# Where the sample groups of a hybrid decoder step keep their states: four buffers, two of them in the GDN chains' scratch memory

## The chip, the cores and the metric

The kernel runs on one core of a Trainium2 chip. The metric is the time of one execution on the device, in microseconds (us): the median over runs. The core has five engines with a queue of instructions each, worked off in order: PE (TensorE, matrix products; the load of a product's stationary side is listed apart as PEld), DVE (VectorE), ACT (ScalarE), POOL (GpSimd), and SP (SyncE), which here issues nearly all DMAs.

## The reference

One layer of a decoder serves two groups of sequences with the same weights: a prompt of 1024 tokens behind 16 learned meta tokens, and 8 samples of one new token each, which carry cached states.

```python
u = rms_norm(x) @ w_in                     # 1024 -> 8216 columns
q_m, k_m, v_m, o_m, z_m, i_m, f_m, q_g, k_g, v_g, z_g, b_g, a_g = split(u)
(C, n, m), hm = chunked(mlstm_chunk, ...)  # 4 heads, state 128 x 256 each
ym = head_rms(hm) * w_mnorm * sigmoid(o_m) * silu(z_m)
qkv = silu(causal_conv(q_g | k_g | v_g))   # width 4
S, og = chunked(gdn_chunk, ...)            # 8 heads, state 128 x 128 each
yg = head_rms(og) * w_gnorm * silu(z_g)
x = x + concat(ym, yg) @ w_out             # 2048 -> 1024
y = rms_norm(x)
```

Both mixers keep a state per head that is handed from chunk to chunk. mLSTM: `C` is scaled by a decay and gets `k` times `v`; the output is `q @ C` and a normaliser. GDN (gated DeltaNet): `S` is scaled by a decay and gets a correction, `k` times (`v` less what `S` holds for `k`), which needs a triangular solve in each chunk. For a sample the chunk is one token: every sample's state (`state_gdn_S`: 8 samples x 8 heads x 128 x 128, `state_mlstm_C`: 8 x 4 x 128 x 256) is read, multiplied with the new `k` and `q`, decayed, changed by one outer product and written back. The outputs are the two groups' rows and all the new states.

## The kernel before

**Work on PE.** The main stream are the projections `u`: tiles of 128 columns of `w_in`, each over three blocks of about 350 tokens, each 24 matmuls of 128 x 350 (weights and input are split into a high and a low part in a fast format, so three products for one). They carry the names `pjg` (GDN), `pjm` (mLSTM), `pjz`, `pjo`, `pjzm` (gates); the generator that emits them is called the filler. At the end comes the output product `op`: seven products of half the size in each direction with 96 matmuls each (a fast matrix scheme, `PRODUCTS`), whose right sides are sums of blocks of `w_out` (`right_sums`: on POOL for the first four, on DVE for the others), split into two parts (`owh` by ACT, `owl` by DVE) and whose results are added into the rows `xr` or `regionxl` on DVE (`drain`). A product's bank is used again two products later, once its additions are done.

**Chains.** Between the projections stand the chains, one head after the other: GDN heads 0 to 7 (`gdn_chain`, products `tp`, `sk`, `up`), then mLSTM heads 0 to 3 (`mlstm_chain`: `mtp`, `mup`, `mnm`), each nine chunks. A step of a GDN chain makes small 128 x 128 tiles in turn: `vt`, `R`, `qs`, `wv`, the state `S`, the output `oo`. Each kind has its own small ring of tiles (`w(tag, ...)`). While a GDN chain runs, `query_squares` squares the head's queries in four pieces on ACT, into the first half of `srow`; DVE transposes each into the second half and sums it.

**Samples.** One generator, `samples`, does the GDN samples and then the mLSTM samples. `gdn_sample` takes the heads in pairs. A state of one head for all 8 samples is a tile of 128 x 1024 (512 KB), and two such tiles are in use, `db` and `ebuf[0]`, which the GDN chains used until then. For a pair: products `sA` of both states with `k` and `q` (16 matmuls, 8 for each state), POOL decays the states, ACT copies the result to `srow`, PE turns it (`sT`), DVE works out the correction, PE turns that (`svt`), it goes to memory and comes back broadcast to all partitions (`vb`), and DVE adds the outer products, 8 instructions for each state. Then `exchange` stores a state and loads the next one into the same tile. `mlstm_sample` does the same in a simpler form with `mqc`, `mqT` and the last sum `mms`, for four heads of two tiles each.

**Weights of the output.** `places` names the memory for the 16 blocks of `w_out` as it comes free: two tiles of the weights' ring, two of the ring `r_gm`, the two `ebuf` once the samples are done, then the region of the input, which is free when the last projection is done.

**What sets the order.** The program is written out by a planner (`Plan`) when it is built. Every generator yields a tile that it waits for, a condition, or an engine, and the planner, with a cost for each instruction and DMA, keeps a clock for each engine and always goes on with the first generator in its list whose wait is over by PE's clock. What comes out is a fixed order for each engine. The waits between engines are semaphores, so at run time an engine stands still where another is later than the planner thought.

Of the kernel before, what the change touches and what calls it, by code (L numbers as in the profile page):

```python
# [286 lines left out]
ORDERS = ((2, 3, 0, 1), (0, 1, 2, 3), (2, 3, 0, 1), (2, 3, 0, 1))  # L287
# [20 lines left out]
def hymba_kernel(ctx: ExitStack, tc: tile.TileContext, a: dict, o: dict):  # L308
# [17 lines left out]
    def room(tag):  # L326
        return plan.room(tag, BANKS[tag])
# [149 lines left out]
    wnames = {}  # L477

# [579 lines left out]
    def gdn_chain(h):  # L1058
# [8 lines left out]
        def prepare(c):  # L1067
# [9 lines left out]
            vt = w("vt", [P], f"vt{h}_{c}")  # L1077
# [11 lines left out]
        for c in range(NCH):  # L1089
# [5 lines left out]
            if c > 0:  # L1095
                pe.matmul(sk[:, P : 2 * P], kc, S, start=True, stop=True)
                pe.matmul(tp[:, 3 * P : 4 * P], qc, S, start=True, stop=True)
                R = w("R", [P], f"R{h}_{c}")
                dve.scalar_tensor_tensor(
                    out=R, in0=sk[:, P : 2 * P], scalar=negc[:, c, h : h + 1], in1=vt, op0=ALU.mult, op1=ALU.add)  # L1100
                qs = w("qs", [P], f"qs{h}_{c}")
# [5 lines left out]
            wv = w("wv", [P], f"wv{h}_{c}")  # L1107
# [7 lines left out]
            Sn = w("S", [P], f"S{h}_{c}", bufs=3)  # L1115
            if c == 0:
                dve.tensor_copy(Sn, up[:, 0:P])
            else:
                dve.scalar_tensor_tensor(
                    out=Sn, in0=S, scalar=egend[:, c, h : h + 1], in1=up[:, 0:P], op0=ALU.mult, op1=ALU.add)  # L1120
                oo = w("oo", [P], f"oo{h}_{c}", 3)
# [32 lines left out]

    def query_norms():

        yield squares
        yield room("k")
        pt = pst2("qsum")
        pe.matmul(pt[:, 0 : 32 * GH], fold, squares.rearrange("p h b -> p (h b)"), start=True, stop=True)  # L1160
        yield pt
        for r in range(4):
            rows = slice(32 * r, 32 * r + 32)
            part = pt[rows, 0 : 32 * GH].rearrange("p (h c r) -> p h c r", h=GH, r=4)[:, :, :, r]
            dve.scalar_tensor_tensor(out=hst[rows, MH : MH + GH, :], in0=part, scalar=EPS * MDK, in1=hst[rows, MH : MH + GH, :], op0=ALU.mult, op1=ALU.add)

    def store(place, o_):

        yield r_gm.can
        turns[0] += 1  # L1170
        ti, turn = r_gm.get([D], f"turn{turns[0]}")
# [9 lines left out]

    turns = [0]
# [31 lines left out]

    def exchange(t, to, source, key):
# [3 lines left out]
        if source is not None:  # L1219
            yield plan.read[t.tensor.name]  # L1220
# [4 lines left out]
    def gdn_sample():  # L1225
# [57 lines left out]
        vbs = ebuf[1], vb  # L1283
        for h in range(0, GH, 2):
            yield lambda: h == 0 or ("sS", h) in done and ("sS", h + 1) in done
            for x in (*sb, kn):
                yield x
            yield room("k")
            at = pst2(f"sA{h}")
            for i in range(2):  # L1290
                for b in range(NS):
                    g, j = divmod(b, 4)
                    g = P * (g + 2 * i)
                    pe.matmul(at[32 * j : 32 * j + 32, g : g + P], knf[:, 16 * h : 16 * h + 32], sb[i][:, b, :], start=True, stop=True)
            for i in range(2):
                pool.tensor_tensor(out=sb[i], in0=sb[i], in1=eg[:, h + i].unsqueeze(2).to_broadcast([P, NS, P]), op=ALU.mult)
            yield at
            for i in range(2):
                act.copy(srow[:, 256 * i : 256 * i + 256], at[:, 256 * i : 256 * i + 256])
            yield srow  # L1300
            yield room("k")
            turned = pst2(f"sT{h}")
            for g in range(4):
                pe.transpose(turned[:, P * g : P * g + P], srow[:, P * g : P * g + P], ident)
            yield turned
            for i in range(2):
                hi = h + i

                def of(k):
                    c = 272 * i + 8 * k  # L1310
                    return turned[:, c : c + 33 * NS - 32 : 33]

                dve.tensor_tensor(out=sn[:, 3, hi], in0=of(0), in1=eg[:, hi], op=ALU.mult)
                dve.scalar_tensor_tensor(out=sn[:, 3, hi], in0=vv[:, hi], scalar=0.5, in1=sn[:, 3, hi], op0=ALU.mult, op1=ALU.subtract)
                dve.tensor_tensor(out=sn[:, 3, hi], in0=sn[:, 3, hi], in1=bet[:, hi], op=ALU.mult)
                dve.tensor_tensor(out=sn[:, 4, hi], in0=of(1), in1=eg[:, hi], op=ALU.mult)
                dve.tensor_tensor(out=sn[:, 5, hi], in0=sn[:, 3, hi], in1=r[:, 5, hi], op=ALU.mult)
                dve.tensor_tensor(out=sn[:, 4, hi], in0=sn[:, 4, hi], in1=sn[:, 5, hi], op=ALU.add)
            yield sn
            yield room("k")  # L1320
            vp = pst2(f"svt{h}")
            pe.transpose(vp[0 : 2 * NS, 0:P], sn[:, 3, h : h + 2].rearrange("p h b -> p (h b)"), ident)
            vsb = wk.tile([2 * NS, P], F32, tag="vsb", name=f"vsb{h}")
            act.copy(vsb, vp[0 : 2 * NS, 0:P])
            sp.dma_start(vb_d[8 * h : 8 * h + 16], vsb)
            for i in range(2):
                sp.dma_start(vbs[i], vb_d[8 * (h + i) : 8 * (h + i) + 8].partition_broadcast(P))
            for i in range(2):
                hi, s_, vb = h + i, sb[i], vbs[i]
                yield s_  # L1330
                yield vb
                for b in range(NS):
                    if b % 2 == 0:
                        yield "dve"
# [914 lines left out]
```

## Time and profile before

| | |
|---|---|
| median of three runs | 1180.1 us (1176.85 to 1181.13) |
| profiled execution | 1178.63 us |
| its span, first to last instruction | 1176.8 us |
| PE busy | 1154.7 us (98%) |
| DVE, ACT, POOL busy | 893.3, 589.0, 466.3 us |
| mean granted clock of PE | 0.997 |
| DMA | 171.63 MB, 146 GB/s in the mean |

An engine's busy time is the time in which an instruction of it ran. PE's matmuls overlap each other and the weight loads, so that busy PE is not PE at its peak. A row of the timeline gives the start from the span's beginning, the duration, the engine, and what was written and read, and in brackets how long the engine had been idle just before and what it waited for. Names are those of the program without numbers. Every instruction carries line 56, that of the recording wrapper, so tiles and not lines tell them apart.

### The profile page before, as it was taken

The numbers are of one execution on the slowest core, as the hardware profiler recorded it, in microseconds if no ns is written. First come the engines' busy times: TensorE is split into PE (matmuls) and PEld (weight loads), VectorE is DVE, ScalarE is ACT, GpSimd is POOL, SyncE is SP. The second block draws the span as 40 slices with busy tenths as digits, with TensorE's granted clock in tenths as the row PEclk, the third lists the DMA queues.
The fourth block names the chain that finished last, engine by engine and source line by source line (L and its number), as shares of the span: only waits on it lengthen the run. The fifth ranks groups of instructions, "written<-read, shape, count | busy, mean of one in ns | idle before, by whom it ended". The sixth has DMA issues, their size and how long they took to land.

```text
span 1176.8 us, 22725 instructions
## 1 busy us (share of the span) xinstructions
PE 1154.7 (98%) x8049; PEld 1080.7 (92%) x8049; DVE 893.3 (76%) x2324; ACT 589.0 (50%) x1814; POOL 466.3 (40%) x644
## 2 busy tenths in 40 slices
PE   8999999999999999999999999999999999989997
PEld 7999999999999999999999989899999999866885
DVE  6789878598887879887664856457868776897886
ACT  6544445566565555655454655456432222433443
POOL 3104877855748295958311341320011111530012
PEclk9999999999999999999999999999999999999999
DMA  6032311313122223022412557667798988873342
GB/s 247 16 101 71 95 51 50 105 55 90 44 81 62 80 66 85 26 69 80 130 69 69 170 179 220 195 208 263 242 342 282 354 303 322 285 257 119 111 157 85
DMA packets 94460, 171.63 MB, mean 146 GB/s; under 512 B 28025, under 2 KB 53841, under 8 KB 94346
## 3 DMA queue, kind: packets, MB, share of 16 engines
q1 hardware_dynamic: 94152, 170.01, 44.0%
q8 instruction: 63, 1.03, 0.4%
q14 instruction: 51, 0.42, 0.1%
q10 hardware_dynamic: 194, 0.17, 0.1%
HBM read 116.04 MB, written 54.10 MB: 145 GB/s over the span
## 4 chain that ended last, share of the span: by engine, by line
PE 82%; DVE 8%; DMA 5%; issue 2%; ACT 1%; SPq 1%; POOL 1%; DVEq 0%; POOLq 0%; ACTq 0%
PE pjg L56 22%; PE pjm L56 10%; PE op L56 9%; PE pjz L56 8%; PE pjo L56 7%; PE pjzm L56 7%; PE up L56 4%; PE tp L56 3%; PE sk L56 2%; PE mnm L56 2%; PE mup L56 2%; PE kk L56 1%; SPq L56 1%; DVE owl L56 1%; PE xtp L56 1%
## 5 line engine op out<-in xcount | busy, mean ns | idle before, releaser
L56 PE MATMUL pjg<-xht,whg 128*128 128x350 f32 (+6 forms) x624 | 197.3, 323 | 1.0 <-ACT xht L56 1.0
L56 PE MATMUL pjg<-xlt,whg 128*128 128x350 f32 (+6 forms) x624 | 196.7, 322 | 0.0
L56 PE MATMUL pjg<-xht,wlg 128*128 128x350 f32 (+6 forms) x592 | 190.3, 325 | 0.0
L56 POOL TENSOR_TENSOR tmp<-B,E 33x31 f32<-33x31 f32 (+15 forms) x248 | 146.8, 592 | 73.8 <-DMA B<-nd 55.0
L56 POOL TENSOR_TENSOR E<-E,tmp 33x31 f32<-33x31 f32 (+15 forms) x248 | 155.7, 628 | 19.4
L56 PE MATMUL op<-owh,left 128*128 128x512 f32 x448 | 141.7, 395 | 4.0 <-DVE xr L56 4.0
L56 PE MATMUL pjm<-xht,whm 128*128 128x350 f32 (+2 forms) x384 | 127.5, 332 | 0.0
L56 PE MATMUL pjm<-xht,wlm 128*128 128x350 f32 (+2 forms) x384 | 126.7, 330 | 0.0
L56 PE MATMUL pjm<-xlt,whm 128*128 128x350 f32 (+2 forms) x384 | 126.1, 328 | 0.0
L56 PEld LDWEIGHTS pjg<-xht,whg 128*128 128x128 f32 x624 | 116.4, 189 | 1.6 <-issue 1.2
L56 PEld LDWEIGHTS pjg<-xlt,whg 128*128 128x128 f32 x624 | 116.4, 189 | 0.4
L56 PEld LDWEIGHTS pjg<-xht,wlg 128*128 128x128 f32 x592 | 110.9, 189 | 0.5
L56 PEld LDWEIGHTS op<-owh,left 128*128 128x128 f32 x448 | 84.1, 188 | 26.7 <-DVE xr L56 5.3
L56 DVE SCALAR_TENSOR_TENSOR kq<-cr,prm,kq 128x346 f32<-128x346 f32 (+7 forms) x147 | 96.2, 660 | 10.8 <-ACT cr L56 5.2
L56 PE MATMUL op<-owl,left 128*128 128x512 f32 x224 | 88.5, 395 | 0.0
L56 POOL TENSOR_TENSOR db<-db,sgb 128x1024 f32<-128x1024 f32 x8 | 15.4, 1922 | 167.2 <-PE mqc L56 90.6
L56 PEld LDWEIGHTS pjm<-xht,whm 128*128 128x128 f32 x384 | 72.8, 190 | 0.6 <-ACT who L56 0.2
L56 PEld LDWEIGHTS pjm<-xht,wlm 128*128 128x128 f32 x384 | 72.7, 189 | 0.5 <-issue 0.2
L56 PEld LDWEIGHTS pjm<-xlt,whm 128*128 128x128 f32 x384 | 72.8, 190 | 0.4 <-issue 0.2
L56 ACT COPY cr<-pjg 128x3 f32<-128x3 f32 (+8 forms) x124 | 40.5, 326 | 51.5 <-PE pjg L56 51.3
L56 PE MATMUL pjz<-xht,wlz 128*128 128x344 f32 x192 | 62.8, 327 | 0.0
L56 PE MATMUL pjz<-xht,whz 128*128 128x344 f32 x192 | 62.8, 327 | 0.0
(367 smaller groups left out, 3126.6 us busy)
## 6 DMA issues: line engine op xcount, KB each, us to landing
wrg<-in_wt SPq DMA_DIRECT2D x23, 512.0 KB, 3.9
left<-c_d SPq DMA_DIRECT2D x40, 256.0 KB, 2.7
wrm<-in_wt SPq DMA_DIRECT2D x16, 512.0 KB, 6.5
h_d<-turn SPq DMA_DIRECT2D x64, 128.0 KB, 3.7
ht<-h_d SPq DMA_DIRECT2D x16, 512.0 KB, 6.4
gm<-rows_d SPq DMA_DIRECT2D x8, 576.0 KB, 5.6
xt<-in_x_p SPq DMA_DIRECT2D x8, 512.0 KB, 5.4
wrz<-in_wt SPq DMA_DIRECT2D x8, 512.0 KB, 3.4
```

Source lines behind the costliest of these rows:

```text
L56: r = f(*args, **kw)
```

## The change

1. One tile `small` of sixteen pieces of 128 x 128 takes the place of the chains' six small rings; `piece(tag)` hands the pieces out in turn, in the same numbers as the rings had. The last two pieces are the second buffer for `query_squares`: its pieces 1 and 3 are written there, 0 and 2 to `srow` as before.
2. When the last GDN chain is done, the first sixteen pieces become two state tiles of 128 x 1024 (`pairs_of_pieces`). `gdn_sample` then runs two lanes: one takes heads 0, 1, 4, 5 through `db` and `ebuf[0]`, the other heads 2, 3, 6, 7 through the two halves of `small`. Each lane has one buffer for the broadcast corrections instead of two for all. `sample_banks` keeps the lanes from holding both PSUM banks of their kind, and `rows_held` gives `srow` to one lane at a time.
3. `mlstm_sample` loads the states of two heads at its start, into the four tiles, and a freed tile gets the state two heads on.
4. `places` names `ebuf[0]`, the two halves of `small` and `ebuf[1]` first, each as soon as the mLSTM samples have left it. Eight blocks instead of ten then go to the input's region.
5. `ORDERS[2]`: mLSTM head 2 projects queries and keys ahead of its values.

```diff
-ORDERS = ((2, 3, 0, 1), (0, 1, 2, 3), (2, 3, 0, 1), (2, 3, 0, 1))
+ORDERS = ((2, 3, 0, 1), (0, 1, 2, 3), (0, 1, 2, 3), (2, 3, 0, 1))
...
+    small = gp.tile([P, 16, P], F32, name="small")
+    plan.split(small, P)
+    plan.war.add(small.tensor.name)
+    PIECES, turns = dict(vt=(0, 2), wv=(2, 2), S=(4, 3), R=(7, 2), qs=(9, 2), oo=(11, 3)), {}
+
+    def piece(tag):
+        first, n = PIECES[tag]
+        turns[tag] = k = turns.get(tag, -1) + 1
+        return small[:, first + k % n, :]
...
-            vt = w("vt", [P], f"vt{h}_{c}")
+            vt = piece("vt")
...
-            sq, turned = srow[:, 0 : 2 * P], srow[:, 2 * P : 4 * P]
+            sq = small[:, 14:16, :].rearrange("p a b -> p (a b)") if i % 2 else srow[:, 0 : 2 * P]
+            turned = srow[:, 2 * P : 4 * P]
...
+    held, rows_held = [0], set()
+    pairs_of_pieces = [small[:, 8 * i : 8 * i + 8, :] for i in range(2)]
+
+    def sample_banks():
+        return held[0] < 2
...
-        sb = (db, ebuf[0])
-        for i in range(2):
-            yield plan.read[sb[i].tensor.name]
-            sp.dma_start(sb[i], a["s_S"][i])
+        def lane(first, sb, vb):
+            for i in range(2):
+                yield plan.read.get(plan.key(sb[i]), 0.0)
+                sp.dma_start(sb[i], a["s_S"][first + i])
+                done.add(("sS", first + i))
+            for h in range(first, GH, 4):
+                yield lambda: ("sS", h) in done and ("sS", h + 1) in done and ("C", GH - 1) in done
...
+                for i in range(2):
+                    hi, s_ = h + i, sb[i]
+                    yield plan.read.get(plan.key(vb), 0.0)
+                    sp.dma_start(vb, vb_d[8 * hi : 8 * hi + 8].partition_broadcast(P))
...
+                    plan.add(exchange(s_, o["s_S"][hi], a["s_S"][hi + 4] if hi + 4 < GH else None, ("sS", hi + 4)))
+            done.add(("lane", first))
+
+        plan.add(lane(0, (db, ebuf[0]), ebuf[1]), SAMPLE)
         yield lambda: ("C", GH - 1) in done and r_gm.can()
         gi, vb = r_gm.get([NS, P], "svb")
         yield plan.read[vb.tensor.name]
...
+        plan.join(small)
+        plan.split(small, D)
+        plan.add(lane(2, pairs_of_pieces, vb), SAMPLE)
+        yield lambda: ("lane", 0) in done and ("lane", 2) in done
...
+        states = db, ebuf[0], *pairs_of_pieces
+        for n in range(4):
+            yield plan.read.get(plan.key(states[n]), 0.0)
+            sp.dma_start(states[n], a["s_C"][n // 2, n % 2])
+            done.add(("sC", n))
...
+            sb = [states[(2 * h + i) % 4] for i in range(2)]
...
-                plan.add(exchange(s_, o["s_C"][h, i], a["s_C"][h + 1, i] if h + 1 < MH else None, ("sC", h + 1, i)))
+                plan.add(exchange(s_, o["s_C"][h, i], a["s_C"][h + 2, i] if h + 2 < MH else None, ("sC", n + 4)))
...
+        for n, t in enumerate((ebuf[0], *pairs_of_pieces, ebuf[1])):
+            yield has("sC", min(9 + n, 11))
+            yield plan.read[plan.key(t)]
+            yield t.rearrange("p a b -> p (a b)")
...
-        yield has("samples")
-        for e in ebuf:
-            yield e.rearrange("p a b -> p (a b)")
```

What moves on the engines, at three places of the written order. First ScalarE, at the start of GDN head 6's chain: the third and fourth square of head 5, the evacuation of a projection, and the first `vt`. Before:

```order
L56 ACTIVATE cr_358_7132<-kq_6598 128x346
L56 ACTIVATE srow<-kq_4976 128x256 x2
L56 ACTIVATE mv_2_7280<-pjm_2_2_7492 128x340
L56 ACTIVATE msam<-pjm_2_2_7492 128x8
L56 ACTIVATE vt_0_7550<-tp_0_7546,kap_6205 16x128
```

And now:

```order
L56 ACTIVATE cr_358_6842<-kq_6344 128x346
L56 ACTIVATE srow<-kq_4806 128x256
L56 ACTIVATE small<-kq_4806 128x256
L56 ACTIVATE mv_2_6980<-pjm_2_2_7187 128x340
L56 ACTIVATE msam<-pjm_2_2_7187 128x8
L56 ACTIVATE small<-tp_0_7241,kap_5960 16x128
```

The places are the same; one of the two squares, and `vt`, are written to other memory.

Second PE, at a pair of heads whose states have been loaded into used tiles. Before, the third pair (heads 4 and 5), amid the projection `pjm` of 128 x 350 and at the start of an mLSTM chain (`mtp_0`, `mup_0`):

```order
L56 MATMUL mtp_0_10104<-ident,mkq_9583 16x128
L56 MATMUL mtp_0_10104<-ident,mv_2_9188 16x128
L56 MATMUL mtp_0_10104<-ident,mv_3_9327 16x128
L56 MATMUL sA_10112<-db,skn 32x128 x8
L56 MATMUL sA_10112<-ebuf_101,skn 32x128 x8
L56 MATMUL pjm_3_0_10095<-xht,wlm_3_10022 128x350
```

And now the second pair of the second lane (heads 6 and 7), in a step of an mLSTM chain; the first lane's second pair stands 32 projection matmuls ahead of it:

```order
L56 MATMUL mup_2_9252<-va_162,mkt_2_9254 128x257
L56 MATMUL mnm_2_9287<-C_1_9248,mwq_8364 128x257
L56 MATMUL mnm_2_9287<-va_162,mpm_2_9258 128x257
L56 MATMUL mtp_3_9296<-ident,mkq_7828 128x128
L56 MATMUL mup_3_9298<-mkq_7828 128x128
L56 MATMUL sA_9316<-small,skn 32x128 x16
```

The products with the states stand at other points of the chains, two pairs closely behind each other, and the second lane's read `small`.

Third DVE, in the output product, at the additions of the first product (`op` of 0 to 3 is the bank) into the rows `regionxl` and `xr`, among splits of the right (`owl`) and left sides. Before:

```order
L56 TENSOR_TENSOR regionxl<-regionxl,op_0_13093 128x512 x2
L56 TENSOR_TENSOR owl_13121<-regionxl,owh_13120 128x512 x2
L56 TENSOR_TENSOR left_10990<-left_10990 128x512
L56 TENSOR_TENSOR regionxl<-regionxl,op_1_13097 128x512
L56 TENSOR_TENSOR owl_13039<-regionxl,owh_13038 128x512 x2
L56 TENSOR_TENSOR xr_1_13307<-xr_1_13307,op_1_13097 128x512
L56 TENSOR_TENSOR xr_2_13309<-xr_2_13309,op_2_13101 128x512
```

And now:

```order
L56 TENSOR_TENSOR regionxl<-regionxl,op_0_12693 128x512 x2
L56 TENSOR_TENSOR left_10695<-left_10695 128x512 x2
L56 TENSOR_TENSOR regionxl<-regionxl,op_1_12697 128x512
L56 TENSOR_TENSOR xr_1_12900<-xr_1_12900,op_1_12697 128x512
L56 TENSOR_TENSOR owl_12583<-regionxl,owh_12582 128x512 x2
L56 TENSOR_TENSOR xr_2_12902<-xr_2_12902,op_2_12701 128x512
L56 TENSOR_TENSOR xr_2_12904<-xr_2_12904,op_2_12701 128x512
```

Two splits now stand behind the additions from the second bank and two others ahead of them.

## Rows read from the trace of the kernel before

**Rows 1.** The page, part 1, TensorE: busy us, share of the span, instructions.

```profile
PE 1154.7 (98%) x8049; PEld 1080.7 (92%) x8049; DVE 893.3 (76%) x2324; ACT 589.0 (50%) x1814; POOL 466.3 (40%) x644
```

**Rows 2.** Waits of PE: who waits <- for whom: us in total, times, longest.

```profile
PE op L56 <- DVE xr L56: 4.0, 3, 2.1
PE up L56 <- ACT vt L56: 1.7, 1, 1.7
PE sA L56 <- DMA ebuf<-in_s_S: 1.3, 1, 1.3
PE mup L56 <- ACT va L56: 1.2, 2, 0.6
PE mqc L56 <- DMA ebuf<-in_s_C: 1.2, 1, 1.2
...
PE mup L56 <- DVE mpm L56: 0.8, 1, 0.8
```

**Rows 3.** Timeline 535.5 to 539, all engines: start, duration (us), instruction, [idle before <- releaser].

```profile
535.61 0.43 DVE L56 STREAM_TRANSPOSE srow<-srow 128x256 f32<-128x256 f32 x1
...
536.07 0.42 ACT L56 ACTIVATE srow<-kq 128x256 f32<-128x256 f32 x1 [2.57 <-DVE srow L56]
...
537.60 0.42 ACT L56 ACTIVATE srow<-kq 128x256 f32<-128x256 f32 x1 [1.11 <-DVE srow L56]
...
538.04 0.45 ACT L56 ACTIVATE mv<-pjm 128x340 f32<-128x340 f32 x1
...
538.45 0.34 ACT L56 ACTIVATE vt<-tp,kap 16x128 f32<-16x128 f32 x1
...
538.85 0.39 PE L56 MATMUL up<-vt,em 16*16 16x128 f32 x2 [1.66 <-ACT vt L56]
```

**Rows 4.** Timeline of PE, 740 to 756: the second head's products, and a projection after.

```profile
744.72 0.65 PE L56 MATMUL sA<-ebuf,skn 128*32 128x128 f32 x16 [1.30 <-DMA ebuf<-in_s_S]
...
748.61 0.49 PE L56 MATMUL pjm<-xlt,whm 128*128 128x350 f32 x1
```

**Rows 5.** Windows, PE: stretch, its length, PE busy (instructions), PEclk, DMA share, GB/s.

```profile
745.00:750.00 5.00, 5.00 (x34) 0.68 0.61 197
750.00:755.00 5.00, 5.00 (x31) 0.98 0.64 203
```

**Rows 6.** Timeline of PE, 658 to 694: waits in the mLSTM chains.

```profile
662.71 0.70 PE L56 MATMUL mup<-va,mkt 128*128 128x257 f32 x2 [0.62 <-ACT va L56]
...
665.22 0.70 PE L56 MATMUL mup<-va,mkt 128*128 128x257 f32 x2 [0.62 <-ACT va L56]
...
690.77 0.67 PE L56 MATMUL mup<-va,mkt 128*128 128x257 f32 x2 [0.83 <-DVE mpm L56]
```

**Rows 7.** Timeline of SyncE, which issues the DMAs, 622 to 748.

```profile
634.86 0.38 SPq L56 DMA_DIRECT2D wrm<-in_wt  x1
657.66 0.33 SPq L56 DMA_DIRECT2D vb_d<-vsb  x1
...
726.80 0.41 SPq L56 DMA_DIRECT2D out_s_S<-ebuf  x1
...
738.54 0.88 SPq L56 DMA_DIRECT2D ebuf<-in_s_S  x1
```

**Rows 8.** Timeline of PE, 1040 to 1056: waits in the output product.

```profile
1047.29 0.50 PE L56 MATMUL op<-owh,left 128*128 128x512 f32 x1 [1.64 <-DVE xr L56]
...
1051.55 0.50 PE L56 MATMUL op<-owh,left 128*128 128x512 f32 x1 [2.09 <-DVE xr L56]
```

**Rows 9.** Timeline of DVE, 985 to 1056.

```profile
1004.20 1.28 DVE L56 TENSOR_TENSOR ht<-mg,yg 128x512 f32<-128x512 f32 x2
...
1025.18 2.90 DVE L56 TENSOR_TENSOR left<-left 128x512 fp32r<-128x512 f32 x1
...
1046.56 1.87 DVE L56 TENSOR_TENSOR xr<-xr,op 128x512 f32<-128x512 f32 x3
```

**Rows 10.** Timeline of POOL, 960 to 1060: one of its sums of output weights.

```profile
1024.99 2.53 POOL L56 TENSOR_TENSOR regionxl<-regionxh 128x1024 f32<-128x1024 f32 x1 [0.29 <-DMA regionxh<-in_wo]
```

More of the change, by code (lines that the diff above doesn't have):

```diff
@@ L1275, in gdn_sample, with of @@
         sn = sqs
-        sb = (db, ebuf[0])
-        for i in range(2):
-            yield plan.read[sb[i].tensor.name]
-            sp.dma_start(sb[i], a["s_S"][i])
+        def lane(first, sb, vb):
[5 more added lines that the diff above has]
+                yield lambda: ("sS", h) in done and ("sS", h + 1) in done and ("C", GH - 1) in done
+                for x in (*sb, kn):
+                    yield x
+                yield lambda: sample_banks()
+                yield room("k")
+                held[0] += 1
+                at = pst2(f"sA{h}")
+                for i in range(2):
+                    for b in range(NS):
+                        g, j = divmod(b, 4)
+                        g = P * (g + 2 * i)
+                        pe.matmul(at[32 * j : 32 * j + 32, g : g + P], knf[:, 16 * h : 16 * h + 32], sb[i][:, b, :], start=True, stop=True)
+                for i in range(2):
+                    pool.tensor_tensor(out=sb[i], in0=sb[i], in1=eg[:, h + i].unsqueeze(2).to_broadcast([P, NS, P]), op=ALU.mult)
+                yield at
+                yield lambda: not rows_held
+                rows_held.add(h)
+                for i in range(2):
+                    act.copy(srow[:, 256 * i : 256 * i + 256], at[:, 256 * i : 256 * i + 256])
+                held[0] -= 1
+                yield srow
+                yield lambda: sample_banks()
+                yield room("k")
+                held[0] += 1
+                turned = pst2(f"sT{h}")
+                for g in range(4):
+                    pe.transpose(turned[:, P * g : P * g + P], srow[:, P * g : P * g + P], ident)
+                rows_held.discard(h)
+                yield turned
+                for i in range(2):
+                    hi = h + i
+                    def of(k):
+                        c = 272 * i + 8 * k
+                        return turned[:, c : c + 33 * NS - 32 : 33]
+                    dve.tensor_tensor(out=sn[:, 3, hi], in0=of(0), in1=eg[:, hi], op=ALU.mult)
+                    dve.scalar_tensor_tensor(out=sn[:, 3, hi], in0=vv[:, hi], scalar=0.5, in1=sn[:, 3, hi], op0=ALU.mult, op1=ALU.subtract)
+                    dve.tensor_tensor(out=sn[:, 3, hi], in0=sn[:, 3, hi], in1=bet[:, hi], op=ALU.mult)
+                    dve.tensor_tensor(out=sn[:, 4, hi], in0=of(1), in1=eg[:, hi], op=ALU.mult)
+                    dve.tensor_tensor(out=sn[:, 5, hi], in0=sn[:, 3, hi], in1=r[:, 5, hi], op=ALU.mult)
+                    dve.tensor_tensor(out=sn[:, 4, hi], in0=sn[:, 4, hi], in1=sn[:, 5, hi], op=ALU.add)
+                held[0] -= 1
+                yield sn
+                yield lambda: sample_banks()
+                yield room("k")
+                vp = pst2(f"svt{h}")
+                pe.transpose(vp[0 : 2 * NS, 0:P], sn[:, 3, h : h + 2].rearrange("p h b -> p (h b)"), ident)
+                vsb = wk.tile([2 * NS, P], F32, tag="vsb", name=f"vsb{h}")
+                act.copy(vsb, vp[0 : 2 * NS, 0:P])
+                sp.dma_start(vb_d[8 * h : 8 * h + 16], vsb)
+                for i in range(2):
+                    hi, s_ = h + i, sb[i]
+                    yield plan.read.get(plan.key(vb), 0.0)
+                    sp.dma_start(vb, vb_d[8 * hi : 8 * hi + 8].partition_broadcast(P))
+                    yield s_
+                    yield vb
+                    for b in range(NS):
+                        if b % 2 == 0:
+                            yield "dve"
+                        dve.scalar_tensor_tensor(out=s_[:, b], in0=vb[:, b], scalar=kn[:, hi, 0, b : b + 1], in1=s_[:, b], op0=ALU.mult, op1=ALU.add)
+                    plan.add(exchange(s_, o["s_S"][hi], a["s_S"][hi + 4] if hi + 4 < GH else None, ("sS", hi + 4)))
+            done.add(("lane", first))
@@ L1282, in gdn_sample @@
         yield plan.read[vb.tensor.name]
[L1283 to L1334, printed above, removed]
-                    dve.scalar_tensor_tensor(out=s_[:, b], in0=vb[:, b], scalar=kn[:, hi, 0, b : b + 1], in1=s_[:, b], op0=ALU.mult, op1=ALU.add)
-                plan.add(exchange(s_, o["s_S"][hi], a["s_S"][hi + 2] if hi + 2 < GH else None, ("sS", hi + 2)))
@@ L1567, in load_values @@
             done.add(("sv", n))
-        for i in range(2):
-            sp.dma_start(sb[i], a["s_C"][0, i])
-            done.add(("sC", 0, i))
         plan.add(load_values(0))
         for h in range(MH):
-            yield lambda: ("sC", h, 0) in done and ("sC", h, 1) in done
+            sb = [states[(2 * h + i) % 4] for i in range(2)]
+            yield lambda: ("sC", 2 * h) in done and ("sC", 2 * h + 1) in done
             for x in sb:
```

26 lines of the change are left out of this document (14 added, 12 removed).

## The prediction

> **What bounds the kernel now.** I read the page first: TensorE is busy 1154.7 of 1176.8 us [rows 1], and no other engine comes near. The kernel is a stream of projections into which a planner drops the short products of the chains and of the samples, so time can only go where PE stands still or runs slowly. The second view was therefore who PE waits for [rows 2]. Its twelve rows add up to 13.8 us, the six shown, which the change can reach, to 10.2. The reader is to see how little that is (1.2% of the span) and that the largest item, 4.0 us in three waits, lies in the output product, behind VectorE's additions into `xr`. The other six are the program's start and single waits of 0.2 us, which the change does not touch. Third, I followed each of the others on the timeline to what came last before it [rows 3, 4, 6, 8], and looked for stretches where the granted clock was below 1 [rows 5]: after the wait in `sA` at 744.7 us it was 0.68 over 5 us, that is part of the time at 1.2 GHz, the lower of the two levels. A lost share of 0.32 x 5 us and 0.02 x 5 us is 1.7 us of work done late.
>
> The order of the instructions shows the same 6877 on PE before and after. On PE they stand in the same places up to the first products with the sample states (about 635 us), where the chain of the last GDN head ends. Up to there only names differ, and who waits for whom. So the sum is made of single waits: which of them go, and which come.
>
> **The change part by part.**
>
> *Squares of the queries in two buffers.* At 538.85 PE waits 1.66 us for `vt`, the first input of GDN head 6's chain [rows 3]. `vt` is late because ScalarE, which works in order, stands 2.57 us before the third square of head 5 (its buffer, half of `srow`, is still being read: the transpose at 535.61 is of the second square) and 1.11 us before the fourth, and then has `mv` and a short copy to do before `vt` at 538.45. With the second and fourth square in the spare end of the new tile, the third need not wait at all, and the fourth only for the transpose that ends at 535.61 + 0.43 = 536.04. The fourth then runs from about 536.05 to 536.45 instead of from 537.60, `vt` starts at 538.45 - 1.55 = 536.9, and PE finds it when it comes at 538.85 - 1.66 = 537.19. I take 1.6 us off. If DVE reached that transpose 1.5 us later than in this execution, nothing would be gained.
>
> *GDN samples in two lanes.* Before, four pairs of heads go through one pair of buffers, so three reloads lie on the way from one pair to the next. In one of them PE has done the first head's products and waits 1.30 us for `ebuf` [rows 4], and the slow clock follows, with projection matmuls of 0.49 us [rows 4, 5]: 1.3 + 1.7 = 3.0 us. After, each lane reloads once, two reloads in all (heads 4 and 5; 6 and 7). One wait in three reloads at 3.0 us is 1.0 us a reload; two would give back 2.0. A lane has, however, the other lane's work between its own steps, so I take 0.5 us each, 1.0 us together, and keep 0 and 2.0 as ends. The 64 multiply-adds on DVE, the 8 scalings on POOL and the DMAs are the same in number and only stand closer together. The loads of the second lane are new in their place: they are issued behind the last `out_p_S`, and PE asks for them one head of four chain steps later. Before, SyncE issued nothing between 634.86 and 657.66 us [rows 7], so I cost them at nothing; that cover would be gone if the last `oo` were stored late.
>
> *mLSTM samples two heads ahead.* Of PE's waits, 1.2 us is `mqc` waiting for `ebuf` to be loaded [rows 2]. With four buffers a reload has a whole head's work more to land in. I take the 1.2 off, and nothing comes back.
>
> *What moves with them.* The mLSTM chains of heads 1 and 2 start some 100 and 70 projection matmuls later, and head 2 now projects queries and keys first. Before, the end of head 0's chain ran two steps with no projection between, since the next projection waited for the chain's value tiles: 0.62 us twice [rows 6]. After, one such place is left (the last step of head 1), so 0.6 us goes. The other kind in the same rows, 0.83 us behind DVE, comes wherever DVE has transposes and splits before a chain's product; with the samples' DVE work denser I add 1.2 us for it (one and a half such waits; ends 0 and four, 3.3 us).
>
> *Output weights sooner.* The first four blocks of `w_out` go to `ebuf` and the new tile as soon as the mLSTM samples leave them, before the last projections. The samples end some 260 projection matmuls earlier. For PE this matters through DVE, which is filled from the last gate to the third product. In the order, from the last projection's evacuation to the additions that the waiting steps need, DVE has 46 instructions before and 38 after for the second bank, 48 and 42 for the third, 51 and 47 for the fourth: work of gate 6 has moved ahead of the output product, and two splits stand behind the second bank's addition instead of ahead of it. One such instruction is 0.6 us where nothing blocks it (1.28 us for two [rows 9]). So the additions come 4.8, 3.6 and 2.4 us sooner. PE lost 1.64 us at the second bank and 4.0 us in all by the fourth [rows 2, 8]: the first two waits go, and of the 4.0 us by the fourth at most 4.0 - 2.4 = 1.6 us stays. I take 1.0 us as left, 3.0 off; ends 4.0 off and 2 added.
>
> A row of the trace speaks against this part. A subtraction of this size, some 0.6 us, took 2.90 at 1025.18 [rows 9], and POOL was in one of its sums from 1024.99 to 1027.52 [rows 10]: DVE stood until POOL was done, 2.2 us. The Trainium skill says the same of this pair ("SBUF — State Buffer", section "SBUF: two separate sides"): the shared port pair is "an exclusive lock, not a bandwidth split", and a DVE instruction with two inputs in SBUF blocks fully against a GpSimd one that reads SBUF. By that rule, sums whose weights are there sooner could stand closer to DVE's work and block it more often; here the row agrees, and what it would cost is the first rival.
>
> **Sum.** Off: 1.6 + 3.0 + 1.2 + 0.6 + 3.0 = 9.4. Added: 1.0 + 1.2 = 2.2. Net 7.2 us against the profiled execution's 1178.6 gives 1171.4. That execution is 1.5 us under the median of the three runs, so against the median 1180.1 it is 1172.9, and I predict 1173.
>
> **Rivals.**
> 1. *POOL's sums take from DVE what the moved work gave.* For it: ten sums on POOL lie beside the first two products, each about 2.5 us long [rows 10], and not all of them hit a DVE instruction before. Two hits more at 2.2 us eat the 2.4 to 4.8 us. The 4.0 us stay or grow by half: instead of 3.0 off, between 0 and 2 added. Against it: their pace is set by the splits of the product before, not by the weights, and their number is the same. Time 1173 + 3 to 5, say 1177.
> 2. *The waits are not removed but dealt anew.* Each wait was a fraction of a microsecond by which a real engine came later than planned; a new order has new ones. For it: the 0.62 and 0.83 us waits have nothing to do with the samples [rows 6]. Against it: `sA`, `mqc` and the squares have a named cause that is gone. Then only the 1.6 and 1.2 go: 1180.1 - 2.8 = 1177.3, up to 1180.
> 3. *Slower: a lane's reload stuck in SyncE's queue.* SyncE issues in order. Before, the store of `ebuf` was issued at 726.80 and its reload at 738.54, 11.7 us behind, because stores that wait for DVE and a weight load stood between [rows 7]. After, the reload of the second lane's last buffer stands behind a weight load and four stores of `turn`, and PE has its products only 32 projection matmuls after the first lane's. If it trails by the same 11.7 us with nothing planned for it, PE stands about 10 us there and, as now, 1.3 at the first lane, each with the slow clock after it (2 x 1.7): 14.7 us in place of the 1.0 taken, 1173 + 13.7 = 1186.7. It decides from a wait of some 10 us on. Against it: the longest wait of PE for any DMA in this trace is 1.3 us [rows 2], and the planner holds the products until its own landing time.
>
> **How the numbers follow.** The forecast has 0.64, with its own range from the ends above: 1173 - 1.0 - 1.2 - 1.0 - a little for the run is 1168.5, and 1173 + 1.0 + 2.1 + 1.0 is 1177. Rivals 1, 2 and 3 have 0.16, 0.10 and 0.08; 0.02 is for what I don't see. What a measurement of this kernel can tell from no change is about 0.5%, 5.9 us: under 1174.2 is faster, over 1186.0 slower. Some five in six of the forecast's cases lie under 1174.2: 0.54 faster. The rest of it and rivals 1 and 2 are no change, 0.36, and 0.10 is slower. The range of 8 in 10 runs from 1167 to 1181, which takes in rivals 1 and 2.
>
> **What would show it.** Right: in the view of PE's waits, no `up` behind `vt` of over 0.3 us, no `mqc` behind a DMA, `sA` behind a DMA at most once, `op` behind `xr` 2 us or less, a sum under 8 us; granted clock 1.00 in all windows of 5 us between 600 and 1000 us; the samples' last product (`mms`) some 260 projection matmuls sooner. Wrong: an `op` wait of 4 us or more with DVE rows of 2.9 us beside it (rival 1), the same sum on other names (rival 2), or an `sA` row with 5 us and more before it and SyncE rows of `turn` ahead of the load (rival 3).

## The result, and the profile after

| | before | after |
|---|---|---|
| median | 1179.5 us (17 runs) | 1170.9 us (17 runs) |
| profiled execution, its span | 1178.6, 1176.8 us | 1171.0, 1169.2 us |

The ratio is 0.9926, with a 95% interval of 0.9911 to 0.9940: the kernel is 0.74% faster, some 8.7 us, where 7.2 were forecast, and 2 us under the 1173 predicted. One of the 17 executions after took 1884.2 us at a mean granted clock of 0.557; the ratio leaves it out. The page of the changed kernel, part 1, and its waits of PE (who waits <- for whom: us in total, times, longest):

```profile
PE 1151.9 (99%) x8049; PEld 1079.4 (92%) x8049; DVE 910.6 (78%) x2324; ACT 587.8 (50%) x1814; POOL 467.6 (40%) x644
```

```profile
PE op L56 <- DVE xr L56: 2.4, 2, 2.0
PE pjo L56 <- ACT to L56: 1.5, 1, 1.5
...
PE pjo L56 <- DVE mg L56: 0.8, 1, 0.8
PE mup L56 <- ACT va L56: 0.7, 1, 0.7
...
PE up L56 <- ACT small L56: 0.2, 1, 0.2
```

Against [rows 2], `vt`, `sA`, `mqc` and three waits of `mup` are gone, one of `mup` has come, `op` has lost 1.5 us, and two waits of `pjo` are new. The view's sum went from 13.8 to 9.1 us.

The place of [rows 3] in the timeline after (start, duration, instruction, [idle before <- releaser]). `small<-tp,kap` is the tile that was `vt`:

```profile
532.10 0.40 ACT L56 ACTIVATE srow<-kq 128x256 f32<-128x256 f32 x1
...
534.30 0.43 DVE L56 STREAM_TRANSPOSE srow<-small 128x256 f32<-128x256 f32 x1
...
534.76 0.42 ACT L56 ACTIVATE small<-kq 128x256 f32<-128x256 f32 x1 [2.26 <-DVE srow L56]
...
535.61 0.34 ACT L56 ACTIVATE small<-tp,kap 16x128 f32<-16x128 f32 x1
...
536.01 0.39 PE L56 MATMUL up<-small,em 16*16 16x128 f32 x2
```

The third square of head 5 (532.10) runs without a wait. The fourth (534.76) waits only for the transpose of the second at 534.30, which reads its buffer, and the chain's tile follows behind `mv` and a short copy, as before. PE has no wait left that the row shows.

The lanes' reloads on SyncE, and the clock in the windows they land in (stretch, length, busy time of each engine, PEclk, DMA share, GB/s), against [rows 5, 7]:

```profile
678.50 0.47 SPq L56 DMA_DIRECT2D out_s_S<-ebuf  x1
...
686.09 0.35 SPq L56 DMA_DIRECT2D ebuf<-in_s_S  x1
...
692.22 0.51 SPq L56 DMA_DIRECT2D out_s_S<-small  x1
699.27 0.35 SPq L56 DMA_DIRECT2D small<-in_s_S  x1
```

```profile
680.00:700.00 20.00, 20.00 (x152) 19.48 (x151) 12.71 (x19) 8.25 (x22) 12.74 (x12) 1.00 0.98 361
700.00:720.00 20.00, 20.00 (x147) 18.00 (x146) 13.41 (x55) 11.61 (x48) 5.74 (x4) 1.00 0.45 130
```

The four reloads are issued 7.1 to 8.5 us behind their stores, against 11.7 before, and PE is busy without a gap all the same, at full granted clock.

The output product: PE first (against [rows 8]), then DVE and POOL (against [rows 9, 10]):

```profile
1041.18 0.50 PE L56 MATMUL op<-owh,left 128*128 128x512 f32 x1 [0.41 <-DVE xr L56]
...
1044.17 0.50 PE L56 MATMUL op<-owh,left 128*128 128x512 f32 x1 [2.03 <-DVE xr L56]
...
1026.38 2.89 DVE L56 TENSOR_TENSOR left<-left 128x512 fp32r<-128x512 f32 x1
...
1026.22 2.50 POOL L56 TENSOR_TENSOR regionxl<-regionxh 128x1024 f32<-128x1024 f32 x1 [4.42 <-DMA regionxh<-in_wo]
```

The DVE row starts beside a sum on POOL and takes 2.2 us longer than the 0.68 of its kind. A row so lengthened is called a hit here. Between 996 and 1042 us DVE has eight such rows; before, between 1004 and 1047 us, it had six, one of them (5.71 us for two instructions) with two hits.

What the prediction did not foresee is in the gates. SyncE, DVE, ACT and PE in order of time, and SyncE's own wait in the stretch 944 to 946:

```profile
936.62 0.33 SPq L56 DMA_DIRECT2D small<-in_wo  x1
937.00 0.42 SPq L56 DMA_DIRECT2D ebuf<-in_wo  x1
937.52 0.38 SPq L56 DMA_DIRECT2D y_d<-y  x1
...
945.66 0.32 SPq L56 DMA_DIRECT2D y<-g_d  x1
946.26 0.32 SPq L56 DMA_DIRECT2D ht<-h_d  x1
...
952.54 1.67 DVE L56 SCALAR_TENSOR_TENSOR y<-ht,wgh,y 128x256 f32<-128x256 f32 x4 [4.71 <-DMA ht<-h_d]
...
954.25 0.62 ACT L56 CAST left<-y 128x512 fp32r<-128x512 f32 x1 [7.51 <-DVE y L56]
954.77 0.45 ACT L56 ACTIVATE to<-pjo 128x344 f32<-128x344 f32 x1
...
955.28 0.43 PE L56 MATMUL pjo<-xht,who 128*128 128x344 f32 x1 [1.52 <-ACT to L56]
```

```profile
SPq L56 <- DMA y_d<-y: 5.9, 1, 5.9
```

Read it upward. PE waits for a bank that ACT must empty (`to<-pjo`). ACT, in order, stands at `left<-y`, which waits for DVE; DVE stands at `y<-ht`, which waits for a load that SyncE issued only at 946.26, since it had stood 5.9 us at a load behind the store `y_d<-y`. That store was issued right behind two blocks of output weights of 512 KB each, and SyncE got past it 8 us later. This row alone does not make the two blocks the cause: in the kernel before, the eight stores `y_d<-y` took 7.9 us in the median from issue to landing, without such blocks. e2 and e9 below tell more.

### The profile page after: what moved, and what is told of

It is laid out like the page before. It is cut to its first block, busy times and chain, and to the rows that moved or that the text cites. A ratio compares the mean times of both kernels' runs of the same rounds, so it can differ in the third digit from the quotient of the medians.

```text
span 1169.2 us, 22728 instructions
## 1 busy us (share of the span) xinstructions
PE 1151.9 (99%) x8049; PEld 1079.4 (92%) x8049; DVE 910.6 (78%) x2324; ACT 587.8 (50%) x1814; POOL 467.6 (40%) x644
## 4 chain that ended last, share of the span: by engine, by line
PE 85%; DMA 6%; DVE 5%; issue 2%; ACT 1%; SPq 1%; POOL 0%; DVEq 0%; ACTq 0%
PE pjg L56 24%; PE pjm L56 15%; PE op L56 9%; PE pjz L56 8%; PE pjo L56 5%; PE pjzm L56 4%; PE up L56 4%; PE tp L56 3%; PE sk L56 2%; PE mnm L56 2%; PE mup L56 2%; PE kk L56 1%; DMA out_s_C<-small 1%; DMA s_d<-ht 1%; DMA ht<-h_d 1%
## 5 line engine op out<-in xcount | busy, mean ns | idle before, releaser
L56 PE MATMUL pjo<-xht,who 128*128 128x344 f32 x192 | 61.9, 322 | 2.3 <-ACT to L56 1.5
```

The lines of the kernel that those rows point to most:

```text
L56: r = f(*args, **kw)
```

## The experiments

All are compared with the kernel before on the same chip. "Waits" is the sum of the view of PE's waits. The runs are from several chips, on which the kernel before had medians from 1177.8 to 1179.5 us, and a run of six executions can hold a late one (e2: 1172.2). So a difference of two medians is good to some 2 us, and the ratios are given beside it where that matters.

| run | median us | ratio to before (95%) | span us | waits us |
|---|---|---|---|---|
| before | 1179.5 | | 1176.8 | 13.8 |
| after | 1170.9 | 0.9926 (0.9911 to 0.9940) | 1169.2 | 9.1 |
| e1 squares alone | 1176.5 | 0.9979 (0.9962 to 0.9995) | 1177.4 | 13.6 |
| e2 weights late | 1165.3 | 0.9896 (0.9870 to 0.9923) | 1164.8 | 5.9 |
| e3 lanes in turn | 1180.8 | 1.0018 (1.0003 to 1.0034) | 1178.7 | 15.8 |
| e4 sums on DVE | 1171.4 | 0.9941 (0.9918 to 0.9964) | 1168.9 | 7.4 |
| e5 e2 and e3 together | 1187.6 | 1.0076 (1.0055 to 1.0097) | 1186.3 | 21.5 |
| e6 e2, mLSTM in two buffers | 1174.5 | 0.9963 (0.9948 to 0.9978) | 1170.8 | 10.3 |
| e7 after, gates with slack | 1173.7 | 0.9952 (0.9936 to 0.9968) | 1173.5 | 10.5 |
| e8 e2, third sums on DVE | 1169.7 | 0.9929 (0.9906 to 0.9951) | 1168.1 | 7.2 |
| e9 two weights early | 1166.9 | 0.9906 (0.9886 to 0.9927) | 1167.4 | 6.6 |
| e10 e2, old order of head 2 | 1174.4 | 0.9970 (0.9957 to 0.9983) | 1174.5 | 13.0 |

**e1, the squares alone**, in the kernel before:

```diff
-            sq, turned = srow[:, 0 : 2 * P], srow[:, 2 * P : 4 * P]
+            sq = spare if i % 2 else srow[:, 0 : 2 * P]
+            turned = srow[:, 2 * P : 4 * P]
```

> The kernel before, with only the squares of the queries in two buffers (the second and fourth go to a spare tile of 256 columns). Theory: the wait of 1.66 us for vt at head 6 goes and nothing else moves before 640 us, so the profiled span is 1.5 us under the kernel before's 1176.8, with its waits for sA, mqc and xr still there. Second part of the theory: the two small waits in the chains before it (at 500 and 510 us, 0.66 us of the difference between the traces) come from the squares as well, since ScalarE is freed there too; then it is 2.2 us. Rival: the part up to 640 us belongs to other edits (the chains' pieces in one tile); then the span is within 0.3 us of 1176.8 and the wait for vt stays over 1 us.

The wait for `vt` is gone, and the median is 2.8 us lower; the order on PE, POOL and SyncE is that of the kernel before. So this term is shown. A wait for `R` of 0.16 us is still there at 508 us, so that one of the two small waits in the earlier chains, at least, belongs to something else. The profiled span did not follow: the time went again at waits far from the squares. Its waits, and three windows:

```profile
PE op L56 <- DVE xr L56: 3.9, 3, 2.1
PE mqc L56 <- DMA ebuf<-in_s_C: 2.4, 1, 2.4
PE sA L56 <- DMA ebuf<-in_s_S: 1.6, 1, 1.6
```

```profile
740.00:750.00 10.00, 8.53 (x53) 7.45 (x54) 4.34 (x12) 2.88 (x13) 9.61 (x10) 0.83 0.72 248
920.00:930.00 10.00, 8.66 (x58) 8.25 (x59) 7.65 (x15) 1.56 (x4) 3.00 (x2) 0.83 1.01 390
1050.00:1060.00 10.00, 9.42 (x34) 7.51 (x35) 8.76 (x15) 3.95 (x7) 0.00 (x0) 0.83 0.48 160
```

The samples' old waits are longer here, and the clock is low behind each of them, also behind `mqc` and `op`, where before it had stayed at 1.00. Nothing was edited there and the order on these engines is the same, so such a wait for a load differs between executions of one order, and `mqc`, 1.2 us before, cost 2.4 + 1.7 here.

**e2, the output weights late**, in the changed kernel: the four early places are taken out of `places`, and both `ebuf` are named after the samples, as before.

```diff
-        for n, t in enumerate((ebuf[0], *pairs_of_pieces, ebuf[1])):
-            yield has("sC", min(9 + n, 11))
-            yield plan.read[plan.key(t)]
-            yield t.rearrange("p a b -> p (a b)")
...
+        yield has("samples")
+        for e in ebuf:
+            yield e.rearrange("p a b -> p (a b)")
```

> The changed kernel, with the output weights loaded as late as before (two blocks to ebuf after the samples, the rest to the region; none to the new tile). Theory: the two new waits in the gates (1.52 us of pjo behind ScalarE at 955 us, 0.76 us behind VectorE at 971 us) come from the two weight blocks that SyncE issues at 936.6 and 937.0 us, which fill the DMA queue ahead of the gates' loads; both waits go, some 2.3 us. In the output product the waits for xr grow from 2.4 us to about 4, as before the change, so the span comes out at 1169.2 - 2.3 + 1.6 = 1168.5 us. Rival: the gates' waits belong to the new places of the mLSTM chains and samples, not to the weights; they stay at about 2.3 us and the span is 1169.2 + 1.6 = 1170.8 us.

The lowest median of all: 5.6 us under the change by the medians, 4.4 by the spans, 3.5 by the ratios, whose intervals just overlap; e9 can't be told from it. The load of the same gate, and what was left of PE's waits for `xr`:

```profile
936.18 0.32 SPq L56 DMA_DIRECT2D ht<-h_d  x1
...
944.00 1.66 DVE L56 SCALAR_TENSOR_TENSOR y<-ht,wgh,y 128x256 f32<-128x256 f32 x4
...
1039.59 0.50 PE L56 MATMUL op<-owh,left 128*128 128x512 f32 x1 [1.85 <-DVE xr L56]
```

The load is issued 10 us sooner, DVE does not wait for it, and no `pjo` or `pjzm` waits. The second half of the theory fell, and that matters more: without early weights `op` waits 1.85 us, not 4. What relieved the output product was not early weights.

**e3, the lanes in turn**, in the changed kernel:

```diff
         plan.split(small, D)
+        yield lambda: ("lane", 0) in done
         plan.add(lane(2, pairs_of_pieces, vb), SAMPLE)
```

> The changed kernel, with the second lane of GDN samples started only when the first is done (four buffers as in the change, but nothing of the other lane between a lane's own two steps). Theory: what removed the wait of sA is the other lane's work between a reload's issue and its use; with the lanes in turn each lane waits at its reload as the kernel before did, once or twice 1.3 us for a DMA at sA and granted clock of about 0.7 in a window of 5 us after each: 1169.2 + 3 to 6 = 1172 to 1175 us. Rival: the planner puts projections there until the reload has landed, and the wait of before was a single misjudged landing; then no sA waits for a DMA and the span stays within 1 us of 1169.2.

Both theories fell. No `sA` waits, as in the rival's first half, yet the span is 9.5 us longer. PE is 3.2 us ahead of the changed kernel at the first output product and has lost 12.5 us by the middle of the third, 11.1 us of waits behind DVE (0.5 of them not shown) against 2.4, the rest at a granted clock of 0.58 and 0.74 in the two windows of 10 us from 1040:

```profile
PE op L56 <- DVE xr L56: 6.6, 2, 5.0
PE op L56 <- DVE regionxl L56: 2.4, 1, 2.4
PE op L56 <- DVE mg L56: 1.6, 1, 1.6
```

The samples' last product runs at 982.7 us instead of 928.0, 9 us ahead of the output product, and the gates' work stands beside it on DVE.

**e5, lanes in turn and weights late**, both edits.

> The changed kernel, with the lanes of GDN samples in turn and the output weights late: the two edits of the runs before together. Theory: what the lanes give is that the samples end 50 us sooner (last product at 928 us instead of 983 us), which clears VectorE before the output product; the output product's waits with the lanes in turn (11.2 us and granted clock of 0.58 and 0.74 in its two windows of 10 us) come from samples that end beside it, whenever the weights are loaded. Then they stay over 4 us here and the span is 1173 us or more, some 9 over the kernel with late weights and two lanes (1164.8). Rival: they come from early weights that meet late samples (sums and loads that wait for the samples' buffers); then late weights bring the waits to those of the kernel before (4.0 us) or less, and the span is about 1167 us (1164.8 + 2.2 for the waits).

The theory holds in its sign, with more than twice the loss. PE waits 11.1 us behind DVE, as in e3, but another 5.9 us, which neither theory had, behind a right side `owh` whose block of weights POOL gets late. Timeline of PE and POOL:

```profile
1000.85 2.34 POOL L56 TENSOR_TENSOR db<-wout,wout 128x1024 f32<-128x1024 f32 x1 [15.48 <-DMA wout<-in_wo]
...
1003.89 0.80 PE L56 MATMUL op<-owh,left 128*128 128x512 f32 x1 [5.91 <-ACT owh L56]
...
1058.09 0.80 PE L56 MATMUL op<-owh,left 128*128 128x512 f32 x1 [8.84 <-DVE xr L56]
```

With samples that end late, early weights save 6.8 us (e3 against e5, medians); with samples that end early, they cost 5.6 (after against e2; 3.5 by the ratios).

**e4, eight sums on DVE**, in the changed kernel; **e8**, the same for the third product alone, in e2 (with `p < 2` and `p >= 2`):

```diff
-                    if p < 4:
+                    if p < 1:
...
-                    for k in range(2 if p >= 4 else 0):
+                    for k in range(2 if p >= 1 else 0):
```

> The changed kernel, with the sums of output weights for the second and third product on VectorE instead of GpSimd (eight sums of 128x1024; the first product's four stay on GpSimd). Theory: VectorE is late with xr since each GpSimd sum that meets one of its instructions holds it up by some 2.2 us (0.68 becomes 2.9); six of the eight hits in this stage are by sums of these two products, 13 us, and the moved work costs 8 x 1.28 = 10 us. VectorE is 3 us earlier by the fourth bank, and the two waits for xr (0.41 and 2.03 us) go: span 1169.2 - 2.4 = 1166.8 us. Rival: VectorE is simply full there, and 10 us more in its queue make xr later: the waits grow by 3 us or more, 1172 us and over.

> The kernel with late output weights, with the four sums of the third product on VectorE instead of GpSimd. Theory: of the hits that hold VectorE up before the one wait left for xr (1.85 us at 1039.6 us), two are by sums of this product (2.6 us instead of 0.7 at 1032.2, 4.1 instead of 1.9 at 1025.2), while the moved sums add 1.28 us each and two of them come after the bank that is waited for: VectorE is 4.1 - 2.6 = 1.5 us sooner there, and the wait falls to about 0.3 us, 1163.3 us. Rival: as in the kernel with the sums of two products on VectorE, the wait moves to a split of the left side (2.8 us): 1164.8 + 1 or more.

In both no wait for `xr` is left, which fits sums on POOL as what made DVE late there; it does not prove it, since the planner dealt out the rest of the order anew. And in both another wait of about that size takes its place, for `left`, and neither run is faster than the kernel it was made from. That is e8's rival; of e4 neither theory saw it. The row of e4:

```profile
1046.08 1.22 PE L56 MATMUL op<-owh,left 128*128 128x512 f32 x2 [2.81 <-DVE left L56]
```

**e6, mLSTM samples in two buffers**, in e2:

```diff
-        states = db, ebuf[0], *pairs_of_pieces
+        states = db, ebuf[0]
...
-                plan.add(exchange(s_, o["s_C"][h, i], a["s_C"][h + 2, i] if h + 2 < MH else None, ("sC", n + 4)))
+                plan.add(exchange(s_, o["s_C"][h, i], a["s_C"][h + 1, i] if h + 1 < MH else None, ("sC", n + 2)))
```

> The kernel with late output weights, with the mLSTM samples back in two buffers (a head's pair is reloaded for the next head, as in the kernel before). Theory: four buffers are what took the wait of mqc away; here mqc waits for a load again, once 1.2 us with no slow clock (as in the kernel before) to 2.4 us and 1.5 us of slow clock after it (as in the kernel with the squares alone): 1164.8 + 1.2 to 3.9 = 1166.0 to 1168.7 us. Rival: with the samples 50 us sooner and nothing else of size on the DMA queue, two buffers are as good: no mqc waits for a DMA, and the span is within 0.5 us of 1164.8.

The theory has the place and the sign, but not the size: the medians differ by 9 us, the spans by 6. PE's timeline, and the window behind:

```profile
920.16 1.08 PE L56 MATMUL mqc<-ebuf,msam 128*32 128x128 f32 x16 [3.96 <-DMA ebuf<-in_s_C]
```

```profile
920.00:930.00 10.00, 9.84 (x60) 9.43 (x61) 9.38 (x21) 2.03 (x5) 2.11 (x1) 0.73 0.85 272
```

4.0 us of wait and 2.7 of slow clock, and a wait of 1.7 us of `pjzm` behind DVE `mg` at 871.7 us that e2 hasn't.

**e7, slack in the gates**, in the changed kernel (early weights kept):

```diff
-        yield ht
+        yield ht, 7.0
```

> The changed kernel with its early output weights, but the planner told that a gate's load lands 4.5 us later than it now assumes, so that the gate's work on VectorE and ScalarE is put behind more of the others'. Theory: the two waits in the gates are ScalarE and VectorE standing at a gate's instruction that waits for a load held up by the weights, with what PE needs queued behind; with the slack these instructions stand behind it instead, and the waits of 1.52 and 0.76 us go although the weights are early: 1169.2 - 2.3 = 1166.9 us, if the output product, which then has the gates' work later, keeps its 2.4 us. Rival: it is not the order behind a late load but the DMA queue itself (PE's own weights late); then the two waits stay. Against the gain: gates that end later could make xr later, by up to 4.5 us.

No `pjo` or `pjzm` waits, though the weights are early: the order behind a late load made the waits. But the price is paid later, as the last sentence feared, 2.5 and 3.3 us in `op`, each with slow clock behind it (0.86 and 0.75 in the two windows of 10 us that hold them):

```profile
PE op L56 <- DVE xr L56: 3.3, 1, 3.3
PE op L56 <- DVE mg L56: 2.5, 1, 2.5
```

**e9, two of the four blocks early**, in the changed kernel:

```diff
-        for n, t in enumerate((ebuf[0], *pairs_of_pieces, ebuf[1])):
+        for n, t in enumerate((ebuf[0], pairs_of_pieces[0])):
```

> The changed kernel, with only the first two of the four blocks of output weights loaded early (those that SyncE issues at 908.9 and 922.6 us); the two of 936.6 and 937.0 us go to the region after the last projections. Theory: the gates' waits come from the two blocks issued back to back at 937 us, just ahead of the gates' loads; with two early blocks the waits of 1.52 and 0.76 us are gone, some 3.6 us by the first output product as with none early, and the rest hangs on the output product (0.4 to 3 us of waits): 1164 to 1168 us. Rival: any early block shifts the gates; then waits of over 1 us stay in pjo or pjzm between 900 and 990 us and the span is about 1169.

The two waits are gone and one of the same chain has come, 12 us behind the place of the first. PE's timeline, and SyncE's wait between 951 and 957 us:

```profile
967.13 0.42 PE L56 MATMUL pjzm<-xht,whzm 128*128 128x344 f32 x1 [2.12 <-DVE mg L56]
```

```profile
SPq L56 <- DMA y_d<-y: 5.5, 1, 5.5
```

So the theory that the pair at 937 us alone does it falls: SyncE stands 5.5 us behind the same kind of store though no output weights were issued just ahead of it. The first block already does harm. SyncE issues the store of the last sample state in `ebuf` within 0.3 us of 899.6 in the changed kernel, e2 and e9; here, in its waits from 898 to 910 us and its timeline, it then stands at the block that goes into the same tile:

```profile
SPq L56 <- DMA out_s_C<-ebuf: 8.4, 1, 8.4
```

```profile
908.64 0.33 SPq L56 DMA_DIRECT2D ebuf<-in_wo  x1
```

The changed kernel stands there 8.7 us, e2 not at all. Behind it are the gates' transfers: the loads `y<-g_d` that e2 issues at 917.2, 933.9 and 950.9 us come at 923.8, 940.9 and 957.0 here. In the changed kernel DVE starts the work for the store `y_d<-y` of 937.5 us at 934.8, and at 929.1 in e2: 5.7 us are lost before the pair at 937 us is issued. And two early blocks cost the gates as much as four: PE starts the output product at 995.3 us here, at 994.5 in the changed kernel and at 990.9 in e2. What the two later blocks add is not shown.

**e10, the old order of mLSTM head 2**, in e2:

```diff
-ORDERS = ((2, 3, 0, 1), (0, 1, 2, 3), (0, 1, 2, 3), (2, 3, 0, 1))
+ORDERS = ((2, 3, 0, 1), (0, 1, 2, 3), (2, 3, 0, 1), (2, 3, 0, 1))
```

> The kernel with late output weights, with the projections of mLSTM head 2 in the order of the kernel before (values first, then queries and keys). Theory: the order removes waits of chain products behind the value tiles; with the old order one or two of 0.6 us come back at the last steps of a chain, and all else stays: 1164.8 + 0.6 to 1.2 = 1165.4 to 1166.0 us. Rival: the order sets when the chain of head 2 and with it the samples behind it can run; then mLSTM samples end tens of projections later and loads and output product meet them, 1168 us or more.

One line of the change is worth 9 us beside two lanes, the size of the rival but not by its way: the samples end at 931.5 us as in e2 (930.9). The loss is in the chains at 659 to 807 us:

```profile
PE mup L56 <- DVE mpm L56: 3.7, 4, 2.4
...
PE mup L56 <- DVE rst L56: 1.4, 1, 1.4
...
PE svt L56 <- DVE wa L56: 0.8, 1, 0.8
```

```profile
660.00:670.00 10.00, 7.79 (x32) 6.47 (x33) 8.50 (x38) 4.14 (x19) 0.00 (x0) 0.83 0.42 123
```

These are mostly chain products behind DVE, the "other kind" for which the prediction added 1.2 us; with the old order it is over 5. DVE has the samples' corrections just ahead of the waits at 659 to 664 us. The longest, 2.4 us at 765, comes after DVE stood 3.5 us at a transpose into `turn`, behind a store of it.

## Why the prediction was right, point by point

- **Squares, 1.6 off: right.** 1.66 became a gap of 0.1, and e1 shows it alone. The way was that foreseen: the third square did not wait, and the fourth only for the transpose of the second.
- **`sA`, 3.0 off, and 1.0 back for the lanes' reloads:** 3.0 off, nothing back. e3 shows that interleaving was not needed for it: with the lanes in turn no `sA` waited either.
- **`mqc`, 1.2 off: right** by the trace of before, but too small for what four buffers can be worth: e1 shows the same wait at 2.4 us with slow clock, e6 at 4.0 with more.
- **Chains, 0.6 off and 1.2 added:** 2.1 off (three waits gone) and 0.7 added. The 0.6 is right, place and all: the two waits behind `va` became one of 0.65 at 726.9 us, the last step of head 1. The 1.2 was wrong in sign: the wait behind DVE went and none of its kind came. e10 shows that this hung on the order of head 2, which the prediction had priced at 0.6.
- **Output weights, 3.0 off: the step that failed.** The waits for `xr` fell from 4.0 to 2.4 us, 1.5 off, and not through the weights: e2 has 1.85 us without early ones, e9 0.2 with two, and with samples that end late e3 and e5 both wait 11.1 us behind DVE, with early weights and with late ones. "The additions come 4.8, 3.6 and 2.4 us sooner" was read from the order of DVE, which all edits had changed together, and put down to one. The early weights themselves cost 4.4 us by the spans (5.6 by the medians, 3.5 by the ratios), 3.6 of it in the gates. The prediction looked for their price in the output product only, not at what the loads would do on the queue that the gates use. Of its rivals, the first (POOL's sums) may have taken part of the gain, with eight hits for seven where it had named two more: in e4 the waits for `xr` vanish with the sums, though the time does not. The second (waits dealt anew) named the kind of thing: 2.3 us in `pjo`.
- **Third rival, a lane's reload stuck in SyncE's queue:** the last reload did trail its store by 7 us, but PE lost nothing there.
- **The signs given in advance.** Kept: no long wait of `up`, no `mqc` and no `sA` behind a DMA, full clock from 600 to 1000 us, samples that end 50 us sooner. Missed: `op` 2.4 us instead of at most 2, and a sum of 9.1 instead of under 8.
- **Two slips without effect.** One of the "single waits of 0.2 us" is 0.4 us (PE behind DVE's `gb`). And the range's upper end, 1177, takes 1.0 us for its last term, while the end named for the output weights, 2 added in place of 3.0 off, would be 5.0.

So the sum came out by compensation, and that it is right to 2 us is in part luck. Its terms off were 9.4, and 2.2 came back; in the trace the same places gave 9.3 off and 0.7 back, the gates cost another 2.6 (with two of 0.1 to 0.2 us in `pjzm`), and 1.1 us came from places that the prediction did not touch (0.45 at the start, where the first input landed sooner, and 0.66 in two small waits of GDN chains at 500 and 510 us, whose cause stays open). That leaves 0.5 us of the 7.6 between the spans, in the output product and the tail, in steps of 0.1 to 0.3 us.

## What to carry to other kernels

Where a planner deals out all waits at once, the price of one part of a change is not in the difference of the two orders: undo each part alone before crediting it. Here undoing the early weights changed the median by -5.6 us (-3.5 by the ratios), putting the lanes in turn by +10; undoing the four mLSTM buffers or the order, in the kernel with late weights, by +9 each (+8 and +9 by the ratios); all of them together are worth -8.7. A load that "may go early" still has a place on a queue: read what it waits for itself, what is issued right behind it, and which engine stands in order behind that.

## What the runs showed of the hardware

- The granted clock behind a wait did not follow the wait's length alone. 1.30 us at `sA` was followed by 0.68 over 5 us [rows 5]; 2.03 us at `op` in the changed kernel by 1.00; 2.5 us in e8 and 2.8 in e4 by 0.83 over 10 us. The three `op` waits that cost nothing more in the kernel before were followed by 0.83 in e1.
- A load into a tile whose store was still under way held SyncE, and all that it had to issue behind: 8.7 and 5.9 us in the changed kernel (`out_s_C<-ebuf`, `y_d<-y`, 512 KB each), 8.4 and 5.5 in e9.
- VectorE beside a sum on POOL: 2.89 us in place of 0.68, in the hits counted above. By the Trainium skill ("SBUF — State Buffer", section "SBUF: two separate sides") the two engines lock each other out of a shared port pair. The traces before and after agree, with 2.2 us a hit. In e4, with eight of the sums off POOL, no product waits for an addition.
